# Low parts of the weights on VectorE, a float32 copy of the S5 result, head squares on TensorE, and q, k, g of the second sequence projected later

## The chip, the cores and the metric

The kernel runs on one core of a Trainium2 chip. The engines are TensorE (PE, its weight loads shown as PEld), VectorE (DVE), ScalarE (ACT), GpSimd (POOL) and SyncE (SP), which issues all the DMA transfers of this kernel. The metric is the device time of one execution in microseconds; less is better.

## What is computed

A trunk of two layers is applied to two sequences of 1024 rows and 1024 features with shared weights. All matrices are float32.

```python
def run(x):
    h = rmsnorm(x, norm_w[0])                       # layer 0
    z, xbc, dt_raw, q, k, v, g = split(h @ w_in_ab)
    y_ssd = ssd_mixer(z, xbc, dt_raw, ...)          # bidirectional, chunks of 128
    y_att = diff_attention(q, k, v, g, ...)         # 8 heads, two softmax maps each
    x = x + concatenate([y_ssd, y_att]) @ w_out_ab
    h = rmsnorm(x, norm_w[1])                       # layer 1
    u, zc = split(h @ w_in_c)
    y = gelu(s5(u))                                 # bidirectional complex scan
    y = y * sigmoid(y @ w_glu + b_glu)
    x = x + (y * silu(zc)) @ w_out_c
    return rmsnorm(x, final_norm_w)
```

In `diff_attention` each head's output is divided by the root of its mean square over 128 features (`o = rmsnorm(o, subln_w)`); that is the place of the squares below.

## The kernel before

**Dense products.** A float32 operand is kept as two parts, a rounded high part (`wh`, `ah`) and the remainder (`wl`, `al`), and a product is the sum of three: high by high, high by low, low by high. `load_w` (line 259) brings a block of 1024 x 512 weights in eight tiles `raw`; ACT makes `wh`, and POOL makes `wl` by a subtraction (line 277), except in the first half of the out-projection, where the weights are scaled and DVE makes it (`split`). With `cols=True` (`w_in_c`, `w_glu`) `raw` is read with a stride. One output tile `dn` of 128 x 512 is 24 matmuls, one block of weights 8 such tiles, 192 matmuls. Activations lie in eight tiles of the tag `act` (names `ac`), 1 MB each; one stage's input fills all of them, and the next stage's load (`load_half`) waits until tiles come free. In `mm_fm` both halves of the rows are in use up to the last column block of the last weights; in `mm_tm` the first half is done earlier.

**Two streams.** `run` (line 1399) writes the work in program order as dense blocks (`with P(bufs, pool)`) and vector stages (`V(...)`). The vector stages get a high priority (VPRIO): setup of the S5 matrices and tables, SSD and heads of sequence one, SSD and heads of sequence two, S5 of one (`s50`, with a low priority), S5 of two (`s51`). They follow each other in the same memory. The dense stream is: in-projection of one (`proj_fm`, `proj_qk` with z, q, k, g, `proj_v`), in-projection of two, out-projection of one (`out0`, a part for the SSD half and one for the attention half), `proj_1` of one, out-projection and `proj_1` of two, then `glu` and `out1` of one, `glu` and `out1` of two. Its results go through staging tiles `ev` of the pools `evd` (5 buffers), `evg` (EVG = 8 buffers, for `glu` and `out1` of one) and `pj`. Buffers of a tag are handed out in the order in which the program makes the tiles.

**The planner.** `Plan` (line 1525) takes all instructions, finds their dependences, and makes one order for each engine by a list schedule with its own costs: at every step the ready instruction with the least priority number goes first. `bonus` (line 1610) takes 10^7 off the number of an instruction that is not on PE and touches a tile `dn_`, `raw_`, `wh_` or `wl_`, so evictions of `dn` and weight preparation go ahead of the vector stages. Each engine then runs its order as it is written, and waits where an input is not there.

**The heads.** For each pair of 128-row blocks `head` (line 761) multiplies by V into `pv` (tag with one buffer), copies it to `oT`, transposes it into a second `pv`, squares the two halves on ACT with an accumulated sum (`sumsq`, tile `junk`), and copies it to `oall`. POOL adds the two softmax maps (`e<-e,e`).

**S5 and the gate.** `s5_unit` (line 1269) handles pairs of groups; after every fourth pair it applies the GELU, splits the result into `wr` and `wl` (which overwrites `w`), and stores both parts to `hT`. `glu` (line 1313) loads both parts as its matmul input, and for each output tile takes three `ev` tiles `y`, `z`, `th`: POOL adds the two parts again into `y` and multiplies by `z`, ACT makes `th` from `dn`, DVE multiplies `y` by it (line 1334) and splits it for the store to `yc`.

Of the kernel before, what the change touches and what calls it, by code (L numbers as in the profile page):

```python
# [27 lines left out]
VPRIO = 1000000  # L28
EVD, EVS, EVG = 5, 6, 8
EB, ACOMB = 4, 2  # L30
HFAST = True
# [23 lines left out]
class Kern:  # L55
# [86 lines left out]

    def rsqrt(self, pool, src, n, mul, add, extra=None, tag="rs", fast=False):

        nc = self.nc
        tag = self.cur["px"] + tag
        x = pool.tile([128, n], F32, tag=tag + "x", name=self.nm("rsx"), bufs=2)
        i_ = pool.tile([128, n], I32, tag=tag + "i", name=self.nm("rsi"), bufs=2)
        y = pool.tile([128, n], F32, tag=tag + "y", name=self.nm("rsy"), bufs=2)
        u = pool.tile([128, n], F32, tag=tag + "u", name=self.nm("rsu"), bufs=2)  # L150
        if extra is None:
# [106 lines left out]

    def load_w(self, w, c0, k0=0, rows=False, cols=False, scale=None, dve=()):


        hi, lo = [], []
        for k in range(8):
# [11 lines left out]
            if scale is None:  # L275
                self.act(hv, raw)
                self.tt(lv, raw, hr, AL.subtract, None if k in dve else self.nc.gpsimd)
            else:
                self.split(raw, hv, lv, scale[:, k:k + 1])
# [152 lines left out]
    def scratch(self, s):  # L432
# [15 lines left out]
        for b in range(8):  # L448
            d["u", b] = self.dt_([8, 16, 8, 128], f"u{s}_{b}")
            d["hT", b] = self.dt_([2, 8, 16, 8, 128], f"hT{s}_{b}")  # L450
        d["hg"] = [[[d["hT", b][x].rearrange("t c i x -> (c i) t x")[:, 4 * hf:4 * hf + 4, :] for b in range(8)]
                    for x in range(2)] for hf in range(2)]
# [72 lines left out]

    def proj_qk(self, s, sl, d):

        w = self.i["w_in_ab"][0]
        for which, c0 in (("z", Z0), ("q", Q0), ("k", K0), ("g", G0)):
            for blk in range(2):  # L530
                ww = self.load_w(w, c0 + blk * 512)
# [229 lines left out]
    def head(self, s, h, d, hp):  # L761
# [30 lines left out]
        for half in range(2):  # L792
# [4 lines left out]
            for t4 in range(4):  # L797
# [43 lines left out]
                for kt in range(8):  # L841
# [5 lines left out]
                    self.mm(pv[:, 0:256], vl, wh, False, kt == 7)  # L847
                oT = hp.tile([128, 256], F32, tag="oT", name=self.nm("oT"), bufs=1)
                self.act(oT, pv[:, 0:256])
                po = self.psv()  # L850
                for t2 in range(2):
                    self.tp(po[:, t2 * 128:t2 * 128 + 128], oT[:, t2 * 128:t2 * 128 + 128])
                for t2 in range(2):
                    self.sumsq(po[:, t2 * 128:t2 * 128 + 128], ssq[:, t4 - 1 + t2:t4 + t2])
                self.act(oall[:, t4 - 1:t4 + 1, :].rearrange("p a b -> p (a b)"), po[:, 0:256])
                if t4 == 1:
                    self.flush()
# [3 lines left out]
    def head_out(self, d, h, half, oall, ssq, s0, hp):  # L861
# [5 lines left out]
        self.stt(s2, sh, EPS, sh, AL.mult, AL.mult)  # L867
        r = self.rsqrt(hp, ssq, 4, 1.0 / 128.0, None, extra=s2, tag="hr", fast=HFAST)
        self.tt(oall, oall, r.unsqueeze(2).to_broadcast([128, 4, 128]), AL.mult)
# [399 lines left out]
    def s5_unit(self, a, q, U, d, sp, between):  # L1269

        nc = self.nc
        for k in range(8):
# [14 lines left out]
            if k % 4 == 3:  # L1287
                for gp in range(2):
                    w = self.ev()
                    self.act(w, ps[gp], AF.Square, scale=math.sqrt(0.044715))  # L1290
                    self.stt(w, w, 1.0, ps[gp], AL.add, AL.mult)
                    self.act(w, w, AF.Tanh, scale=math.sqrt(2.0 / math.pi))
                    self.stt(w, w, 1.0, ps[gp], AL.add, AL.mult)
                    wr, wl = self.ev(F32R), w.bitcast(F32R)
                    self.act(wr, w)
                    self.tt(wl, w, wr.bitcast(F32), AL.subtract)
                    for x, part in enumerate((wr, wl)):
                        self.dma(d["hT", a * 4 + gp * 2 + q][x].rearrange("t c i x -> (t c) i x")[:, k - 3:k + 1, :],
                                 part.rearrange("p (i x) -> p i x", x=128))
# [13 lines left out]
    def glu(self, s, d, big=None):  # L1313
# [7 lines left out]
        for nb in range(2):  # L1321
            ww = self.load_w(self.i["w_glu"][0], nb * 512, rows=True, cols=True)
            for t in range(8):
                hf, cb = t // 4, t % 4
                kf = nb * 4 + cb
                hh, hl = (a[:, cb, :].bitcast(F32) for a in sl[nb][hf])
                y, z, th = self.ev(), self.ev(), self.ev()
                self.dma(z, d["zT", kf][:, hf * 4:hf * 4 + 4, :].rearrange("p t c -> p (t c)"))
                self.tt(y, hh, hl, AL.add, g)
                self.tt(y, y, z, AL.mult, g)  # L1330
# [68 lines left out]
    def run(self):  # L1399
# [12 lines left out]
        @contextmanager  # L1412
        def P(bufs, pool):
            with self.stream(False, pool, bufs):
                yield
# [75 lines left out]
        with work("evd", "right") as ep:  # L1491
# [8 lines left out]
            with P(EVD, ep):  # L1500
                self.s5_T()
                D0(1, self.load_slots(d[1]["xT"]))
                self.out0(0, d[0], 0, xs[0])
            V("ssd1", SS(1))
            with P(EVD, ep):
                self.out0(0, d[0], 1, xs[0], h0)
                self.proj_1(0, d[0], h0)
# [17 lines left out]
class Plan:  # L1525
# [6 lines left out]
    LATE = (250, 0, 0, 0, 0)  # L1532
    DMA0, DMAR, ISSUE = 2300, 0.24, 420

    def __init__(self, tc, nc):
# [74 lines left out]
    def bonus(self, x, acc):  # L1610

        return 10 ** 7 if str(x.engine) != "EngineType.PE" and any(a[0].startswith(("dn_", "raw_", "wh_", "wl_")) for a in acc) else 0

# [258 lines left out]
```

## Time and profile before

| | us |
|---|---|
| median of 3 runs | 3622.99 (3618.75 to 3625.93) |
| profiled execution, its time | 3619.63 |
| profiled execution, its span | 3617.9 |

The span is the time from the first to the last instruction, the time has a little around it. The stages overlap; by the issues of their transfers the vector stages stand about here:

| stage of the vector stream | us from the start | dense work beside it |
|---|---|---|
| S5 matrices and tables | 150 to 570 | in-projection of one |
| SSD of one | 570 to 1015 | in-projection of one and two |
| heads of one | 1015 to 1600 | q, k, g, v of two |
| SSD of two | 1600 to 2050 | out-projection of one, start of `proj_1` |
| heads of two | 2050 to 2650 | `proj_1` of one, out-projection of two |
| S5 of one | 2650 to 2970 | out-projection of two, `proj_1` of two |
| S5 of two | 2975 to 3252 | end of `proj_1` of two, start of `glu` of one |
| none | 3252 to 3618 | `glu` and `out1` of one, then of two |

A row of the stages shows for each engine its busy time and the number of instructions, then PEclk, the TensorE clock that was granted as a share of 2.4 GHz, the mean busy share of the 16 DMA engines and what they moved. A row of a group shows the line, engine, operation, output and inputs, shape and count, then the busy time and the mean of one in ns, then the idle time of the engine before it with what ended that. A row of the timeline shows start, length, engine, instruction and how many of it in a row, in brackets the idle time before it.

### The profile page before, as it was taken

The page shows a single profiled execution, that of the slowest core. Times are in us where ns is not written, and L with a number is a line of the kernel's source. Part 1 is how long each engine was busy: PE and PEld are TensorE (multiplying, and loading weights), DVE is VectorE, ACT ScalarE, POOL GpSimd, SP SyncE. Part 2 cuts the span into 40 slices and gives each one's busy share as a digit, 9 for nine tenths or more (in the row PEclk, how much of TensorE's full clock was granted, in tenths as well). Part 3 has the DMA queues.
Part 4 walks back from the last instruction along what each step waited for, and adds up shares of the span by engine and source line. Part 5 has one row for each costly group of instructions (what it writes and reads, how often), then busy time and mean ns, then how long its engine had stood idle before and what let it go on. Part 6 is the DMA issues. An engine that isn't in the chain of part 4 may idle for free.

```text
span 3617.9 us, 52707 instructions
## 1 busy us (share of the span) xinstructions
PE 3291.4 (91%) x17206; PEld 2678.9 (74%) x17206; DVE 2605.3 (72%) x5393; ACT 1887.7 (52%) x3563; POOL 1019.6 (28%) x781
## 2 busy tenths in 40 slices
PE   6999999999999999998987899999897998659899
PEld 5776788767778888886666678888676787557677
DVE  5488888767857776767788757777758967983243
ACT  4333323447657777744466577776645555443231
POOL 2121223121224444430010144433411112115471
PEclk9999999999999999999997999999998999779999
DMA  5646766886656555449986465686387659758752
GB/s 191 167 136 190 239 209 207 305 285 218 185 158 186 173 172 170 145 155 329 304 282 218 137 168 155 185 243 191 120 277 234 208 186 286 228 186 276 205 171 70
DMA packets 609619, 737.34 MB, mean 204 GB/s; under 512 B 104409, under 2 KB 374361, under 8 KB 609305
## 3 DMA queue, kind: packets, MB, share of 16 engines
q1 hardware_dynamic: 609344, 733.98, 64.8%
q8 instruction: 137, 2.24, 0.3%
q14 instruction: 138, 1.12, 0.1%
HBM read 491.57 MB, written 246.42 MB: 204 GB/s over the span
## 4 chain that ended last, share of the span: by engine, by line
PE 64%; DVE 12%; DMA 6%; ACT 4%; issue 3%; POOL 2%; SPq 1%; DVEq 0%; POOLq 0%; ACTq 0%
PE dn L113 44%; PE q L113 8%; PE pv L113 5%; PE tr L131 3%; PE tr L113 2%; DVE m L116 2%; DMA raw<-in_w_in_ab_dram 2%; DVE b L116 2%; POOL wl L116 1%; SPq L110 1%; DVE E L119 1%; DVE m L1257 1%; DMA raw<-in_w_in_c_dram 1%; PE pv L131 1%; ACT ev L128 1%
## 5 line engine op out<-in xcount | busy, mean ns | idle before, releaser
L113 PE MATMUL dn<-ac,wh 128*128 128x512 f32 x4288 | 1390.7, 401 | 41.1 <-ACT wh L128 26.8
L116 POOL TENSOR_TENSOR wl<-raw,wh 128x512 fp32r<-128x512 f32 x368 | 550.7, 1511 | 1544.1 <-PE dn L113 861.7
L113 PEld LDWEIGHTS dn<-ac,wh 128*128 128x128 f32 x4288 | 806.8, 191 | 223.8 <-ACT wh L128 32.8
L113 PE MATMUL dn<-ac,wl 128*128 128x512 f32 x2144 | 853.8, 401 | 10.6 <-POOL wl L116 10.5
L113 PE MATMUL dn<-wh,ac 128*128 128x512 f32 x1792 | 586.1, 403 | 37.4 <-DVE ev L116 21.0
L113 PEld LDWEIGHTS dn<-ac,wl 128*128 128x128 f32 x2144 | 407.1, 190 | 110.1 <-POOL wl L116 22.4
L128 ACT ACTIVATE e<-e,st 128x1024 f32<-128x1024 f32 x384 | 437.8, 1150 | 67.7 <-DVE st L820 43.3
L116 POOL TENSOR_TENSOR e<-e,e 128x1024 f32<-128x1024 f32 x128 | 308.2, 2408 | 513.0 <-ACT e L128 400.6
L113 PEld LDWEIGHTS dn<-wh,ac 128*128 128x128 f32 x1792 | 341.8, 193 | 122.3 <-DVE ev L116 25.3
L128 ACT ACTIVATE wh<-raw 128x512 fp32r<-128x512 f32 x368 | 274.8, 752 | 263.7 <-DMA raw<-in_w_in_ab_dram 125.0
L128 ACT ACTIVATE ev<-dn 128x512 f32<-128x512 f32 (+2 forms) x252 | 157.3, 627 | 406.2 <-PE dn L113 394.8
L113 PE MATMUL dn<-wl,ac 128*128 128x512 f32 x896 | 361.9, 405 | 3.4 <-DVE wl L119 1.6
L113 PE MATMUL q<-K,Q 128*128 128x512 f32 x1024 | 315.7, 407 | 4.7 <-DVE st L820 3.0
L820 DVE CUSTOM_DVE_ANT_0 e<-q,Tb 128x512 f32<-128x512 f32 x256 | 175.2, 684 | 85.2 <-PE q L113 52.4
L820 DVE CUSTOM_DVE_ANT_0 e<-q,Tb,st 128x512 f32<-128x512 f32 x256 | 191.3, 747 | 38.2 <-PE q L113 20.0
L116 DVE TENSOR_TENSOR wT<-tr,wT 128x512 fp32r<-128x512 f32 x256 | 171.2, 685 | 64.0 <-ACT wT L128 63.3
L113 PE MATMUL pv<-wT,V 128*128 128x256 f32 x1536 | 207.9, 284 | 0.5 <-ACT wT L128 0.3
L113 PEld LDWEIGHTS q<-K,Q 128*128 128x128 f32 x1024 | 179.5, 190 | 38.3 <-DVE st L820 8.1
L113 PEld LDWEIGHTS pv<-wT,V 128*128 128x128 f32 x1536 | 198.9, 190 | 10.4 <-ACT wT L128 1.2
L113 PEld LDWEIGHTS dn<-wl,ac 128*128 128x128 f32 x896 | 172.7, 193 | 45.5 <-POOL wl L116 5.0
L128 ACT ACTIVATE wT<-tr 128x512 fp32r<-128x512 f32 x256 | 149.4, 597 | 100.5 <-PE tr L131 99.2
L128 ACT ACTIVATE G<-P,dt 128x128 f32<-128x128 f32 x512 | 158.7, 389 | 28.1 <-DVE dt L119 10.4
(287 smaller groups left out, 4872.6 us busy)
## 6 DMA issues: line engine op xcount, KB each, us to landing
raw<-in_w_in_ab_dram SPq DMA_DIRECT2D x208, 256.0 KB
Q<-q SPq DMA_DIRECT2D x512, 64.0 KB
tab<-TAB SPq DMA_DIRECT2D x64, 384.0 KB
Tb<-bh_d SPq DMA_DIRECT2D x32, 704.0 KB
q<-ev SPq DMA_DIRECT2D x64, 256.0 KB
k<-ev SPq DMA_DIRECT2D x64, 256.0 KB
v<-ev SPq DMA_DIRECT2D x64, 256.0 KB
ab<-acs SPq DMA_DIRECT2D x32, 512.0 KB
```

Of the source, the lines that this page charges most:

```text
L110: self.nc.sync.dma_start(out=out, in_=in_)
L113: self.nc.tensor.matmul(out, lhsT=l, rhs=r, start=start, stop=stop)
L116: (eng or self.nc.vector).tensor_tensor(out=out, in0=a, in1=b, op=op)
L119: self.nc.vector.scalar_tensor_tensor(out=out, in0=a, scalar=sc, in1=b, op0=op0, op1=op1)
L128: self.nc.scalar.activation(out=out, in_=in_, func=func, **kw)
L131: self.nc.tensor.transpose(out, in_, self.ident[:n, :n])
L820: nc.vector.tensor_tensor_reduce(out=et[:, kc], in0=sp, in1=Tb[:, x0 + kh * 512:x0 + kh * 512 + 512], op0=AL.add, op1=AL.min, scale=1.0, s ...
L1257: nc.vector.tensor_tensor_scan(out=fl(m[:, x]), data0=fl(tab[:, 2]), data1=fl(b[:, x]), initial=0.0, op0=AL.mult, op1=AL.add)
```

## The change

`wl` is made on DVE for all weights. The S5 result is also stored in float32 (`hf`), with `wl` in a tile of its own, and `glu` loads it in place of the addition on POOL. In the heads POOL squares `oT` into `o2`, PE sums its columns with a vector of ones into two spare columns of the transposed tile, and ACT copies the sums. The in-projection of sequence two is split: `proj_fm`, z and v come first, then the SSD half of the out-projection of one; the input is loaded again, and q, k, g follow, written behind the SSD of two. EVG is 14 in place of 8, a helper's small tiles in the heads have one buffer in place of two, and the planner's `bonus` also holds for every instruction not on PE that touches a tile of `evd`, `evg` or `pj`.

```diff
-EVD, EVS, EVG = 5, 6, 8
+EVD, EVS, EVG = 5, 6, 14
 ...
                 self.act(hv, raw)
-                self.tt(lv, raw, hr, AL.subtract, None if k in dve else self.nc.gpsimd)
+                self.tt(lv, raw, hr, AL.subtract)
 ...
+            d["hf", b] = self.dt_([8, 16, 8, 128], f"hf{s}_{b}")
 ...
-    def proj_qk(self, s, sl, d):
+    def proj_qk(self, s, sl, d, what="zqkg"):
 ...
         for which, c0 in (("z", Z0), ("q", Q0), ("k", K0), ("g", G0)):
+            if which not in what:
+                continue
 ...
-                oT = hp.tile([128, 256], F32, tag="oT", name=self.nm("oT"), bufs=1)
+                oT, o2 = (hp.tile([128, 256], F32, tag="oT", name=self.nm("oT"), bufs=2) for _ in range(2))
                 self.act(oT, pv[:, 0:256])
+                self.tt(o2, oT, oT, AL.mult, g)
 ...
                 for t2 in range(2):
-                    self.sumsq(po[:, t2 * 128:t2 * 128 + 128], ssq[:, t4 - 1 + t2:t4 + t2])
+                    self.mm(po[:, 256 + t2:257 + t2], o2[:, t2 * 128:t2 * 128 + 128], self.ones[:, 0:1], True, True)
                 self.act(oall[:, t4 - 1:t4 + 1, :].rearrange("p a b -> p (a b)"), po[:, 0:256])
+                self.act(ssq[:, t4 - 1:t4 + 1], po[:, 256:258])
 ...
-                    wr, wl = self.ev(F32R), w.bitcast(F32R)
+                    wr, wl = self.ev(F32R), self.ev(F32R)
                     self.act(wr, w)
                     self.tt(wl, w, wr.bitcast(F32), AL.subtract)
-                    for x, part in enumerate((wr, wl)):
-                        self.dma(d["hT", a * 4 + gp * 2 + q][x].rearrange("t c i x -> (t c) i x")[:, k - 3:k + 1, :],
+                    blk = a * 4 + gp * 2 + q
+                    for dst, part in ((d["hT", blk][0], wr), (d["hT", blk][1], wl), (d["hf", blk], w)):
+                        self.dma(dst.rearrange("t c i x -> (t c) i x")[:, k - 3:k + 1, :],
                                  part.rearrange("p (i x) -> p i x", x=128))
 ...
-                hh, hl = (a[:, cb, :].bitcast(F32) for a in sl[nb][hf])
                 y, z, th = self.ev(), self.ev(), self.ev()
-                self.tt(y, hh, hl, AL.add, g)
+                self.dma(y.rearrange("p (t x) -> p t x", x=128),
+                         d["hf", kf].rearrange("t c i x -> (c i) t x")[:, t4, :])
                 self.tt(y, y, z, AL.mult, g)
 ...
-                D0(1, self.load_slots(d[1]["xT"]))
+                s1 = self.load_slots(d[1]["xT"])
+                self.proj_fm(1, s1, d[1])
+                self.drain(self.proj_qk(1, s1, d[1], "z"))
+                self.proj_v(1, s1, d[1])
                 self.out0(0, d[0], 0, xs[0])
             V("ssd1", SS(1))
             with P(EVD, ep):
+                s1 = self.load_slots(d[1]["xT"])
+                self.drain(self.proj_qk(1, s1, d[1], "qkg"))
                 self.out0(0, d[0], 1, xs[0], h0)
 ...
+    DENSE = ("_evd_", "_evg_", "_pj_")
 ...
     def bonus(self, x, acc):
-        return 10 ** 7 if str(x.engine) != "EngineType.PE" and any(a[0].startswith(("dn_", "raw_", "wh_", "wl_")) for a in acc) else 0
+        if str(x.engine) == "EngineType.PE":
+            return 0
+        for a in acc:
+            t = self.tiles.get(a[0])
+            if a[0].startswith(("dn_", "raw_", "wh_", "wl_")) or t is not None and any(
+                    k in str(t.cap_key) for k in self.DENSE):
+                return 10 ** 7
+        return 0
```

## Rows read from the trace of the kernel before

**Rows 1.** Page, part 1: busy us, share of the span, instructions.
```profile
PE 3291.4 (91%) x17206; PEld 2678.9 (74%) x17206; DVE 2605.3 (72%) x5393; ACT 1887.7 (52%) x3563; POOL 1019.6 (28%) x781
```
**Rows 2.** Stages: PE, PEld, DVE, ACT, POOL busy (count), clock, DMA share, GB/s.
```profile
1015.00:1600.00 585.00, 577.03 (x3203) 493.36 (x3202) 408.39 (x1082) 406.37 (x781) 246.39 (x140) 1.00 0.54 165
...
1800.00:2050.00 250.00, 200.54 (x1135) 153.78 (x1136) 214.85 (x422) 152.03 (x339) 39.05 (x24) 0.85 0.73 232
...
2650.00:2940.00 290.00, 259.89 (x1400) 221.46 (x1399) 247.49 (x417) 159.32 (x253) 47.24 (x30) 0.94 0.73 237
...
3070.00:3236.00 166.00, 93.72 (x482) 84.15 (x482) 154.99 (x270) 75.50 (x125) 12.19 (x8) 0.74 0.65 211
3236.00:3440.00 204.00, 179.32 (x730) 141.69 (x731) 70.58 (x97) 60.74 (x102) 107.08 (x164) 0.92 0.76 239
3440.00:3618.00 178.00, 167.70 (x719) 135.63 (x718) 74.47 (x146) 48.31 (x86) 78.63 (x62) 0.98 0.36 118
```
**Rows 3.** Waits of POOL from 3070 to 3250: us in total, times, longest.
```profile
POOL ev L116 <- DMA yc<-ev: 145.0, 1, 145.0
```
**Rows 4.** Timeline of the second S5: single lines of ACT, DVE and SP.
```profile
3086.67 1.27 ACT L128 ACTIVATE ev<-dn,gb 128x512 f32<-128x512 f32 x2 [2.39 <-PE dn L113]
...
3238.11 1.28 DVE L119 SCALAR_TENSOR_TENSOR ev<-ev,ev 128x512 f32<-128x512 f32 x2
...
3251.58 0.45 SPq L110 DMA_DIRECT2D hT<-ev  x1
```
**Rows 5.** Stages of the tile `dn` alone: PE, PEld, (DVE,) ACT busy (count).
```profile
3070.00:3236.00 166.00, 14.24 (x54) 10.32 (x54) 0.00 (x0) 1.27 (x2) 0.74 0.65 211
...
3437.00:3618.00 181.00, 169.82 (x722) 136.94 (x722) 10.97 (x16) 10.88 (x16) 0.97 0.38 121
```
**Rows 6.** Timeline near 440 and 460: POOL's low parts and DVE's table products.
```profile
439.21 5.12 POOL L116 TENSOR_TENSOR wl<-raw,wh 128x512 fp32r<-128x512 f32 x3 [3.38 <-ACT wh L128]
439.73 1.77 DVE L116 TENSOR_TENSOR tab<-tab 128x512 f32<-128x512 f32 x1
...
460.44 0.69 DVE L116 TENSOR_TENSOR tmp<-tab 128x512 f32<-128x512 f32 x1
```
**Rows 7.** Stages of the tile `m` on DVE alone: busy (count), clock, DMA.
```profile
2650.00:2940.00 290.00, 167.65 (x271) 0.94 0.73 237
3100.00:3236.00 136.00, 98.66 (x187) 0.73 0.60 194
```
**Rows 8.** Groups of DVE, 2650 to 2940, then 3100 to 3236: a PSUM reader.
```profile
L119 DVE SCALAR_TENSOR_TENSOR ev<-ev,q 128x512 f32<-128x512 f32 x28 | 19.1, 683 | 6.1 <-ACT ev L128 6.0
...
L119 DVE SCALAR_TENSOR_TENSOR ev<-ev,q 128x512 f32<-128x512 f32 x20 | 13.6, 681 | 1.1 <-ACT ev L128 1.1
```
**Rows 9.** Groups of the whole span, shapes kept apart: busy us, mean ns.
```profile
L116 POOL TENSOR_TENSOR wl<-raw,wh 128x512 fp32r<-128x512 f32 x368 | 550.7, 1511 | 1544.1 <-PE dn L113 861.7 <-ACT wh L128 375.4 <-issue 142.4
...
L119 DVE SCALAR_TENSOR_TENSOR uz<-ev,dn 128x512 f32<-128x512 f32 x16 | 17.1, 1079 | 28.5 <-ACT ev L128 28.3
```
**Rows 10.** Stages of POOL's low parts `wl`: POOL busy (count), clock, DMA.
```profile
150.00:1015.00 865.00, 184.25 (x120) 0.98 0.67 211
1800.00:2050.00 250.00, 39.05 (x24) 0.85 0.73 232
2650.00:2940.00 290.00, 47.24 (x30) 0.94 0.73 237
```
**Rows 11.** Group of the squares in the heads, whole span.
```profile
L128 ACT ACTIVATE junk<-pv 128x128 bf16<-128x128 f32 x128 | 34.9, 273 | 8.4 <-PE pv L131 6.0
```
**Rows 12.** Timeline near 768: one-column matmuls on PE.
```profile
768.23 1.05 PE L113 MATMUL tr<-ones,zh 128*128 128x1 f32 x8 [0.25 <-ACT zh L128]
```
**Rows 13.** Stages with the fullest DMA, columns as in the stages above.
```profile
1750.00:1850.00 100.00, 83.05 (x423) 57.99 (x422) 76.84 (x141) 45.03 (x100) 13.31 (x8) 0.91 0.96 321
...
3050.00:3100.00 50.00, 36.35 (x185) 29.71 (x185) 39.57 (x51) 21.33 (x32) 21.51 (x13) 0.86 0.98 290
```
**Rows 14.** Chain that ended last, 2300 to 2360: start, us, what.
```profile
2332.86 12.57 DMA ac<-ys
```

More of the change, by code (lines that the diff above doesn't have):

```diff
@@ L141, in c4, with rsqrt @@
         return t
-    def rsqrt(self, pool, src, n, mul, add, extra=None, tag="rs", fast=False):
+    def rsqrt(self, pool, src, n, mul, add, extra=None, tag="rs", fast=False, bufs=2):
         nc = self.nc
         tag = self.cur["px"] + tag
[L147 to L150, printed above, removed]
+        x = pool.tile([128, n], F32, tag=tag + "x", name=self.nm("rsx"), bufs=bufs)
+        i_ = pool.tile([128, n], I32, tag=tag + "i", name=self.nm("rsi"), bufs=bufs)
+        y = pool.tile([128, n], F32, tag=tag + "y", name=self.nm("rsy"), bufs=bufs)
+        u = pool.tile([128, n], F32, tag=tag + "u", name=self.nm("rsu"), bufs=bufs)
         if extra is None:
@@ L257, in tick, with load_w @@
             self.queue.pop(0)()
-    def load_w(self, w, c0, k0=0, rows=False, cols=False, scale=None, dve=()):
+    def load_w(self, w, c0, k0=0, rows=False, cols=False, scale=None):
         hi, lo = [], []
@@ L867, in head_out @@
         self.stt(s2, sh, EPS, sh, AL.mult, AL.mult)
-        r = self.rsqrt(hp, ssq, 4, 1.0 / 128.0, None, extra=s2, tag="hr", fast=HFAST)
+        r = self.rsqrt(hp, ssq, 4, 1.0 / 128.0, None, extra=s2, tag="hr", fast=HFAST, bufs=1)
         self.tt(oall, oall, r.unsqueeze(2).to_broadcast([128, 4, 128]), AL.mult)
@@ L1325, in glu @@
                 kf = nb * 4 + cb
-                hh, hl = (a[:, cb, :].bitcast(F32) for a in sl[nb][hf])
                 y, z, th = self.ev(), self.ev(), self.ev()
-                self.dma(z, d["zT", kf][:, hf * 4:hf * 4 + 4, :].rearrange("p t c -> p (t c)"))
-                self.tt(y, hh, hl, AL.add, g)
+                t4 = slice(hf * 4, hf * 4 + 4)
+                self.dma(z, d["zT", kf][:, t4, :].rearrange("p t c -> p (t c)"))
+                self.dma(y.rearrange("p (t x) -> p t x", x=128),
+                         d["hf", kf].rearrange("t c i x -> (c i) t x")[:, t4, :])
                 self.tt(y, y, z, AL.mult, g)
```

## The prediction

> **What bounds the kernel now.** I read the shares of busy time first [rows 1]: PE is busy in 91% of the span, DVE in 72%, ACT in 52%, POOL in 28%. An average over stages with different limits says little, so the second view is the table of stages [rows 2]. Three kinds of stage stand in it. In the first sequence's heads (1015 to 1600) PE is busy 577 of 585 us at clock 1.00: every cycle added to PE there is paid, and nothing else is. In the second SSD and in the first S5 (1800 to 2050 and 2650 to 2940) DVE is the fullest engine (215 of 250, 247 of 290). And from 3070 to 3236 PE is busy 94 of 166 us at a granted clock of 0.74, while DVE is at 155 of 166. That last stage is the odd one: work for PE is there, since `glu` and `out1` of sequence one still stand ahead, but of their matmuls only 54 run in it [rows 5].
>
> The waits say why [rows 3]: POOL waits once for 145.0 us until a store `yc<-ev` has landed. The timeline gives the chain [rows 4]: the two first tanh evictions of `glu` run on ACT at 3086.67, but the next step of the same tiles, the multiplication on DVE (line 1334), starts only at 3238.11, when the second S5 has almost left the queue. `bonus` (line 1612) lifts only instructions that touch `dn_`, `raw_`, `wh_` or `wl_`; the eviction reads `dn`, the multiplication and the split after it touch `ev` alone, so the plan put them behind all of the S5's DVE work. With 8 buffers and three `ev` tiles for each step the third step gets none, and PE stands still as far as `glu` goes for as long.
>
> **The change part by part.** The sum is made against the profiled execution: its span is 3617.9, its time 3619.6, and the median of the runs shown, 3623.0, lies 3.4 above that.
>
> *The planner's bonus for `ev` tiles, EVG 14.* The multiplication and the split of `glu` now go ahead of the S5 on DVE, so `glu` and `out1` of sequence one (4 blocks of 192 matmuls, 768 less the 54 already run) move into the stage that starts at 3070. What is late next? DVE: the second S5 needs the 182 us until its last store at 3251.58 [rows 4], and the moved blocks bring 32 evictions of `glu` and 48 of `out1` at 0.69 [rows 6], 55 us, and 32 low parts (below), 28 us: 265 us, the end at 3335. PE: 714 matmuls at 169.82/722 = 0.235 us [rows 5] are 168 us, and the S5's 79 us at clock 0.74 [rows 2, 5] are 59 at full clock, 65 for 182 us: 233 us, so PE is not the bound. DMA: 0.65 of 182 us for the S5 and 0.76 of the 188 us that are left of the next stage [rows 2] are 118 + 143, and the change adds 8.4 MB here (16 stores and 16 loads of 256 KB), 26 us at 211 GB/s per 0.65: 287 us of full engines. The fullest rows show 0.96 and 0.98 [rows 13], so 302 us at 0.95: the end at 3372. DMA ends last by this, DVE 37 us before it. Then comes the tail that needs the second S5: 181 us for `glu` and `out1` of sequence two [rows 5] and about 8 us for the last store and load. 3372 + 189 = 3561 against 3618 is a gain of 57, with the DVE end instead 94. I take 60, near the DMA end, because 0.98 was measured right in this place, from 3050 to 3100.
>
> The same bonus reaches the stores, loads and norm steps of the other dense stages. From 1800 to 2050 PE idles 49 us [rows 2]; the DVE time there is needed all the same, so I count 10 us of it and bound it by 0 and 35.
>
> *Low parts on DVE.* 368 instructions leave POOL, 1.51 us each in the mean [rows 9]. On DVE 272 of them cost the 0.69 of a 128x512 instruction from SBUF, and 96 with a strided side (the input of `w_in_c` and `w_glu`) 1.08, as `uz<-ev,dn` takes it [rows 9]; the trace has no such subtraction on DVE, and the bounds are 0.69 and the 1.51 of POOL. That is 188 + 104 = 292 us more for DVE. Against it stands what POOL takes from DVE now: with POOL on low parts a `tab` instruction takes 1.77, without 0.69 [rows 6]. The two S5 stages measure it: from 2650 to 2940 POOL is busy 47 us [rows 2] with 30 low parts [rows 10], and the instructions on `m` take 167.65/271 = 0.619; with POOL empty they take 98.66/187 = 0.528 [rows 7]. 271 x 0.091 = 25 us, 0.82 per low part, is given back against 0.69 to 1.08 paid. In the stages that DVE limits I count nothing; elsewhere PE covers it, and if that cover goes it is some 30 us in each stage of heads. The Trainium skill, SBUF — State Buffer, "Who interferes with whom", says that VectorE with two inputs in SBUF and a GpSimd instruction that reads SBUF share a read interface, and that the loser blocks for the whole instruction. The trace agrees in kind: `ev<-ev,q`, which reads PSUM, takes 0.683 beside POOL and 0.681 without [rows 8]. By that rule each low part could give back its whole 1.51 us, 45 us instead of 25 in that stage.
>
> *Squares on PE.* ACT loses 128 squares of 273 ns with their accumulator reads [rows 11], 35 us and more, and gets 64 small copies. POOL gets 64 products of 128x256, some 0.75 us each if half of a low part. PE gets 128 matmuls of one column; eight of that shape take 1.05 us [rows 12], 0.13 each: 17 us at most. Half of them fall in the heads where PE has 8 us idle, and count: +8, bounds 0 and 17. New waits: PE's column matmul waits for POOL, where the heads' additions `e<-e,e` of 128x1024 stand ahead; `psv` has one buffer, so the next product with V waits behind it. Low parts that no longer stand on POOL pay for that; 0.
>
> *S5 result also in float32.* 32 additions leave POOL in `glu`, 32 loads and 32 stores of 256 KB come on SP's queue and are counted in the DMA sum for sequence one; for sequence two the load lies under PE work (DMA share 0.36 from 3440 on [rows 2]). The separate low tile takes three of the S5's six `ev` buffers in place of two, used once in four pairs of groups; 0.
>
> *q, k, g of sequence two later.* 6 blocks go behind `out0(0,0)`: 48 weight loads, 80 stores and their evictions change places with 16 weight loads, 16 loads and 16 stores, and SP issues 8 more loads (8.4 MB) of the normalised input. Against: the reload lies in the heads, where DMA is at 0.54 [rows 2]; but the handover from `g` to the attention half is now of the kind where both halves of the input are in use until the last column block, as at 2332.86, where the load of `ys` holds the chain for 12.57 us [rows 14]: +12. For: where `out0(0,0)` stands now DMA is at 0.96 [rows 13], and the load of `ys` with `out0`'s traffic (21 MB) gives way to the stores of k and g (15 MB); 6 MB at 321 GB/s are 19 us, of which I count 10. Net +2, bounds -18 and +15. The heads of sequence two read q, k and g only after the SSD that begins then, so nothing waits for them.
>
> Sum: -60 - 10 + 0 + 8 + 2 = -60; 3619.6 - 60 = 3559.6, and 3.4 up to the median is 3563, rounded to **3560**, with 3525 to 3600 for this case by the bounds.
>
> **The rivals.** (a) DMA does not bind the overlapped stage and the bonus fills the SSD stage too: 34 us and 25 us more, 3500. For it: 0.95 is my figure, the rows go to 0.98. Against: DVE is at 86% in that SSD already, and the plan never packs every transfer. (b) DVE becomes the bound: in the stages to 1015, from 1800 to 2050 and from 2650 to 2940 stand 120 + 24 + 30 = 174 low parts [rows 10], and the V work (S5 setup, SSD, S5) has to wait for each. If little comes back from POOL, 174 x 0.79 (292/368) = 137 us lengthen the chain, and the kernel ends near 3700, slower. It decides from a relief under 0.45 us per low part on, where 174 x 0.34 eats the 60; rows 7 measure 0.82 for one stage. (c) The starvation stays: the float32 load stands late in SP's order, or the three tiles are still handed out in turn and the S5 keeps DVE. Then 60 are missing: 3620. Against it: rows 4 name the instruction, and it now has the bonus. (d) Each low part on POOL holds DVE for all of its 1.51 us [rows 9], so the same 174 give back 0.69 more each than rows 7 say, 120 us: 3440. The lock on the page SBUF — State Buffer of the Trainium skill ("Who interferes with whom") would give that. Rows 7 speak against it.
>
> **How the numbers follow.** Chances: the forecast 0.61, (a) 0.17, (b) 0.09, (c) 0.09, (d) 0.04. The range from 3485 to 3615 takes in the forecast, most of (a), and leaves out (b), (d) and most of (c). Faster by over 0.2% (what a measurement of this kernel can tell from no change) is the forecast, (a), (d) and a third of (c): 0.85; slower is (b): 0.09; 0.06 remain.
>
> **What would show it.** Right: in the second S5 the matmuls of `dn` run through, the 145 us wait of POOL is gone, DMA there is above 0.9, the clock above 0.9; DVE's `m` instructions take 0.53 in both S5; POOL is busy under 600 us. Wrong: the second S5 ends before 3300 or after 3420; `dn` waiting for DVE's `wl` for tens of us; `tr` or `pv` in the heads waiting for POOL's product; strided low parts near 1.5 us. What makes the forecast wrong most easily is the plan itself: it is made anew from all priorities, and every queue's order with it.

## The result and the profile after

The changed kernel takes 3524.5 us in the median (3520.9 to 3532.3), the kernel before, run beside it, 3623.8: a ratio of 0.9731, 95% interval 0.9712 to 0.9750. The forecast was 3560 with a range from 3485 to 3615. The gain is 99 us where 60 were forecast; the time lies inside the range, and the sections below are about the other 39 us. The profiled execution has a span of 3519.1 us, 98.8 under that of before.

The shares of busy time of the changed kernel, to be held against [rows 1]:

```profile
PE 3284.7 (93%) x17462; PEld 2677.3 (76%) x17462; DVE 2652.7 (75%) x5761; ACT 1859.3 (53%) x3371; POOL 483.3 (14%) x445
```

PE has 256 matmul records more and is busy 7 us less; POOL has lost more than half of its work; DVE has taken 368 instructions and is busy only 47 us more. Span less PE's busy time is PE's idle time: 326.5 us before, 234.4 after. So 92 of the 99 us are idle time of PE, and the tables below are read with that sum.

The stages of the changed kernel (columns as in [rows 2]): heads of one, second SSD, first S5, second S5, tail. Each stretch is cut at this kernel's own loads and stores, so that it is the same work as the stage of before, at another time:

```profile
974.00:1574.00 600.00, 590.57 (x3312) 503.32 (x3312) 435.60 (x1147) 385.86 (x669) 194.52 (x112) 0.99 0.61 191
1756.00:2004.00 248.00, 223.98 (x1285) 171.57 (x1285) 207.60 (x440) 154.94 (x364) 0.00 (x0) 0.91 0.77 246
2616.00:2928.00 312.00, 282.92 (x1502) 239.48 (x1502) 269.17 (x477) 172.10 (x271) 0.59 (x6) 0.93 0.73 240
2931.00:3332.00 401.00, 339.29 (x1716) 284.71 (x1714) 311.29 (x516) 184.41 (x300) 59.89 (x120) 0.93 0.92 299
3332.00:3519.00 187.00, 173.89 (x738) 139.93 (x738) 79.68 (x167) 47.91 (x86) 24.33 (x24) 0.97 0.43 135
```

The same cut in the kernel before gives 2970 to 3252 for the second S5 and 366 us of tail. The tile `dn` alone, of before (first fence, those two stretches) and after:

```profile
2970.00:3252.00 282.00, 97.49 (x385) 71.25 (x384) 11.72 (x11) 9.73 (x16) 0.83 0.74 235
3252.00:3618.00 366.00, 335.06 (x1405) 267.47 (x1403) 21.93 (x32) 18.32 (x27) 0.96 0.58 182
```

```profile
2931.00:3332.00 401.00, 266.85 (x1076) 199.36 (x1074) 23.83 (x28) 18.01 (x28) 0.93 0.92 299
3332.00:3519.00 187.00, 173.89 (x738) 139.93 (x738) 11.05 (x16) 10.96 (x16) 0.97 0.43 135
```

That is the starvation of [rows 5], gone: 1076 dense matmuls run beside the second S5 in place of 385, at a clock of 0.93 in place of 0.83, and the tail is 187 us, with 189 forecast. But the whole vector chain also stands earlier: the first S5 load is issued at 2616 instead of 2652 us. The forecast's terms for what lies ahead of the S5 (-10, +8 and +2) add up to nothing. Here it is in the SP lines of before and of after:

```profile
2651.67 0.49 SPq L110 DMA_DIRECT2D mi<-MIN  x1
```

```profile
2615.95 0.32 SPq L110 DMA_DIRECT2D mi<-MIN  x1
```

### The profile page after: what moved, and what is told of

The parts are those of the page before. It is cut to its first block, busy times and chain, and to the rows that moved or that the text cites. A ratio compares the mean times of both kernels' runs of the same rounds, so it can differ in the third digit from the quotient of the medians.

```text
span 3519.1 us, 52816 instructions
## 1 busy us (share of the span) xinstructions
PE 3284.7 (93%) x17462; PEld 2677.3 (76%) x17462; DVE 2652.7 (75%) x5761; ACT 1859.3 (53%) x3371; POOL 483.3 (14%) x445
## 4 chain that ended last, share of the span: by engine, by line
PE 70%; DVE 13%; DMA 7%; ACT 5%; issue 3%; SPq 1%; POOL 0%; DVEq 0%; ACTq 0%; POOLq 0%
PE dn L113 48%; PE q L113 9%; PE pv L113 5%; PE tr L131 4%; PE tr L113 2%; DMA raw<-in_w_in_ab_dram 2%; DVE wl L116 2%; ACT wh L128 1%; DVE m L116 1%; DVE b L116 1%; PE pv L131 1%; SPq L110 1%; DVE E L119 1%; ACT ev L128 1%; DVE ev L119 1%
## 5 line engine op out<-in xcount | busy, mean ns | idle before, releaser
L116 DVE TENSOR_TENSOR wl<-raw,wh 128x512 fp32r<-128x512 f32 x368 | 290.9, 801 | 119.2 <-ACT wh L128 78.8
L113 PE MATMUL q<-K,Q 128*128 128x512 f32 x1024 | 325.5, 409 | 2.8 <-DMA Q<-q 1.1
```

The costliest lines, as they stand in the source:

```text
L113: self.nc.tensor.matmul(out, lhsT=l, rhs=r, start=start, stop=stop)
L116: (eng or self.nc.vector).tensor_tensor(out=out, in0=a, in1=b, op=op)
```

## The experiments

The disputed steps are four: whether the low parts on VectorE cancel (term 0), what the bonus does outside the second S5 (term -10), the squares (term +8), and whether the transfers bound the overlapped stage. "S5 start" below is the issue of the first `mi<-MIN`, "tail" the time from the last `hT` store to the end. Each run had its own executions of the kernel before beside it, whose medians lie between 3625.2 and 3627.5; the interval given is that of the ratio to them. By these intervals a difference under some 10 us between two runs is not settled.

### Low parts: undone, alone, twice, on both engines

Undone in the changed kernel:

```diff
-                self.tt(lv, raw, hr, AL.subtract)
+                self.tt(lv, raw, hr, AL.subtract, self.nc.gpsimd)
```

> The changed kernel with one edit undone: all 368 low parts of the weight blocks are computed by GpSimd again, none by VectorE. Theory A (the low parts on VectorE are what lets the vector chain reach the S5 stage 39 us earlier, 2611 us instead of 2650, because a VectorE operation that runs beside a GpSimd one is held): the first S5 operation comes back to about 2650, the excess of VectorE from GpSimd overlap rises from about 102 us towards 303, and the time is 3550 to 3585 us. Theory B, that of the prediction (what VectorE gains by the relief it pays back by executing the low parts, term 0; the 39 us come from the bonus and the moved projections): S5 still starts within 10 us of 2611 and the time is 3515 to 3535 us.

Measured: 3570.6 us (0.9845, 0.9824 to 0.9866), 46 over the changed kernel, S5 start 2652. All three signs of theory A are there; the excess of VectorE beside GpSimd, explained below, is 286 us.

The kernel before with that one edit in the other direction (`None if k in dve else self.nc.gpsimd` taken out of line 277):

> The kernel before with one edit: all low parts on VectorE. Theory A (low parts bring the vector chain forward by about 39 us): S5 starts at 2605 to 2625 us instead of 2650, the second S5 half still starves the dense work (the wait of dn there stays), and the time is 3570 to 3600 us. Theory B (the prediction's term 0: relief equals cost): S5 starts within 10 us of 2650 and the time is 3610 to 3635 us.

Measured: 3566.5 us (0.9833, 0.9818 to 0.9847), 59 under before, S5 start 2610. The time lies 3.5 us under theory A's range, which is within the noise. Its tail is still 366 us (3200 to 3566), so the starvation is untouched. Theory A holds in both directions: the low parts bring the vector chain forward. Theory B, the prediction's zero, falls.

Then the two prices by themselves. In the changed kernel each low part a second time on VectorE:

```diff
                 self.tt(lv, raw, hr, AL.subtract)
+                self.tt(lv, raw, hr, AL.subtract)
```

> The changed kernel with a cost doubled: each of the 368 low parts is computed twice by VectorE, one after the other into the same tile, some 291 us of VectorE more. The prediction's step held that this work and the relief from GpSimd cancel because VectorE binds, so the cost C of one set of low parts on VectorE would be near 200 us of path or more: 3700 to 3815 us. Theory A' (the low parts mostly fill VectorE's idle time beside the dense work, while a GpSimd operation holds up whatever VectorE has, the short operations of the chain too): C is 10 to 70 us, so 3534 to 3594 us, and the relief is C plus the 46 us that separate the kernel with the low parts on GpSimd from the changed one.

Measured: 3759.1 us (1.0362, 1.0344 to 1.0379). One set of low parts on VectorE costs 3759 - 3524 = 235 us of path. So theory A' falls: these instructions do not sit in idle time. The prediction's view that VectorE binds in most places where they stand holds. And once more on GpSimd instead (`self.tt(lv, raw, hr, AL.subtract, self.nc.gpsimd)` as the second line):

> The changed kernel with all 368 low parts computed by VectorE and then once more, into the same tile, by GpSimd: the GpSimd work of before and the VectorE work of the changed kernel together. If the price of one set on VectorE (C = 235 us by the kernel that computes them there twice) and the price of one set on GpSimd (R, by what it takes from VectorE) add up, then R = C + 46 = 281 and the time is 3790 to 3820 us. If C is convex (the second set costs more than the first because the idle time of VectorE is used up by then), R is smaller: with R of 80 to 200 the time is 3600 to 3725 us. If GpSimd's work costs VectorE nothing and the 46 us were the shorter wait for the low part, 3560 to 3580 us.

Measured: 3806.5 us (1.0500, 1.0473 to 1.0527), 282 over the changed kernel, where the sum of the two earlier runs gave 281. The prices add up within the noise: a set of low parts costs 282 us on GpSimd and 235 on VectorE. The short wait for a low part as the only cause, the third case, is excluded: it wanted 3560 to 3580. How long TensorE waits for a low part stands in these rows (us in total, times, longest), of the changed kernel, the one with the low parts on GpSimd, the one with both sets on VectorE, and the one with a set on either engine:

```profile
PE dn L113 <- DVE wl L116: 9.6, 6, 4.5
...
PE dn L113 <- POOL wl L116: 14.5, 27, 2.0
...
PE dn L113 <- DVE wl L116: 38.4, 45, 3.6
...
PE dn L113 <- POOL wl L116: 54.5, 52, 4.0
```

Undoing the edit lengthens this wait by 5 us, of the 46. In the two kernels with a second set it is longer by 29 and 45 us. So that much of the 235 and of the 282 is a wait for the later result and not time taken from VectorE; some 206 and 237 are left.

The groups of the low parts show where GpSimd's price is paid. The changed kernel, the kernel with both sets on VectorE, and the kernel with a set on either engine (busy us, mean ns | idle before, releaser):

```profile
L116 DVE TENSOR_TENSOR wl<-raw,wh 128x512 fp32r<-128x512 f32 x368 | 290.9, 801 | 119.2 <-ACT wh L128 78.8 <-PE dn L113 35.1 <-DMA mi<-MIN 1.2
```

```profile
L116 DVE TENSOR_TENSOR wl<-raw,wh 128x512 fp32r<-128x512 f32 x736 | 582.1, 809 | 122.7 <-ACT wh L128 68.4 <-PE dn L113 41.0
```

```profile
L116 POOL TENSOR_TENSOR wl<-raw,wh 128x512 fp32r<-128x512 f32 x368 | 589.8, 1611 | 1661.0 <-DVE wl L116 806.8 <-ACT ev L128 211.9 <-ACT G L128 160.6
L116 DVE TENSOR_TENSOR wl<-raw,wh 128x512 fp32r<-128x512 f32 x368 | 381.6, 1049 | 143.3 <-ACT wh L128 94.3 <-PE dn L113 36.1 <-DMA V<-v 4.6
```

The same 368 VectorE instructions take 290.9 us alone and 381.6 beside GpSimd's. I summed, over all VectorE instructions that overlap one on GpSimd, what each takes above the median of its shape without overlap: 102 us in the changed kernel and 405 with a set on either engine, 303 / 368 = 0.82 us for each GpSimd low part. [rows 7] gave the same value from the instructions on `m` in one stage.

PE pays twice for added waiting. With both sets on VectorE its 17462 matmuls are the same, but:

```profile
PE 3364.7 (90%) x17462; PEld 2717.7 (72%) x17462; DVE 2957.0 (79%) x6129; ACT 1864.5 (50%) x3371; POOL 478.7 (13%) x445
```

Of 239 us more span 159 are idle time of PE, and 80 are the same matmuls taking longer, the mean granted clock being 0.943 instead of 0.965.

### The bonus: taken out, alone, for one pool alone, with fewer buffers

```diff
-    DENSE = ("_evd_", "_evg_", "_pj_")
+    DENSE = ()
```

> The changed kernel without the scheduling bonus for the evd, evg and pj tiles (the evg pool still has 14 buffers). The prediction's theory (the bonus is what keeps the second S5 half from starving the dense work): between the second half's start and its last store the dn matmuls are few again, the tail after the last hT store is near 350 us instead of 187, and the time is 3584 to 3625 us (60 to 100 more than 3524). Rival (the 14 buffers or the earlier vector chain do it alone): the tail stays below 220 us and the time is 3520 to 3545 us.

Measured: 3593.5 us (0.9907, 0.9892 to 0.9922), 69 over the changed kernel. The tile `dn` in this kernel's second S5 and tail:

```profile
2941.00:3226.00 285.00, 116.53 (x457) 85.69 (x457) 12.80 (x12) 11.86 (x19) 0.84 0.80 255
3226.00:3591.00 365.00, 327.91 (x1355) 260.27 (x1354) 22.02 (x32) 17.08 (x25) 0.94 0.63 199
```

It is the starvation of before again, buffers or not, so the prediction's theory holds in the changed kernel. What nobody expected is the S5 start: 2565 us, 51 earlier than with the bonus. The bonus delays the vector chain.

The kernel before with the bonus and the 14 buffers alone:

> The kernel before with the bonus for the three tile groups and the evg pool of 14 buffers, and nothing else of the change. The prediction's theory (the bonus carries the gain, all other parts sum to zero): 3550 to 3570 us. Theory A (the bonus removes the starvation of the second S5 half only, the 39 us of earlier S5 need the low parts on VectorE): S5 starts at 2640 to 2655 us, the end lies 55 to 65 below before, also near 3560; so the start of S5 tells the two apart from theory C (the bonus brings both, S5 starts near 2611 and the time is 3515 to 3535 us).

Measured: 3608.6 us (0.9952, 0.9934 to 0.9971), a gain of 17. The S5 starts at 2676, 24 later than before; the stretch from there to its last store grows from 600 to 745 us, the tail falls from 366 to 186. The tail is what was forecast, and most of what it gains is lost ahead of it. None of the three theories said so. Between this run and the first one (3571), which adds the other edits but not the low parts, lie 38 us that no run divides. They are the squares, the move and the float32 copy together; undone in the changed kernel, below, the same three come out as a loss of 17. So what a part is worth depends on the others.

The bonus for `evg` alone, on top of the kernel with the squares on ScalarE (3495 us, below):

```diff
-    DENSE = ("_evd_", "_evg_", "_pj_")
+    DENSE = ("_evg_",)
```

> The kernel with the squares on ScalarE again (3495 us), and the bonus for the evg tiles alone, not for evd and pj. Theory (the evg part ends the starvation in the second S5 half, while the evd and pj parts delay the vector chain ahead of it, 2565 against 2616 us for the first S5 operation without and with the bonus): S5 starts 20 to 50 us earlier than 2589, the tail after the last S5 store stays near 187 us, and the time is 3455 to 3485 us. Rival (what the vector chain gains, the dense work loses, since PE is at 93%): S5 starts earlier, the stretch to its last store grows as much, and the time is 3490 to 3520 us.

Measured: 3467.0 us (0.9566, 0.9543 to 0.9589), S5 start 2571, tail 189. The S5 starts 18 us earlier, just short of the 20 expected, and the stretch from there to its last store doesn't grow, as the rival has it, but falls from 716 to 701 us. So the `evd` and `pj` parts of the bonus cost 28 us, and the `evg` part alone ends the starvation. This is the fastest kernel of the study, 160 us under before and 57 under the change:

```profile
PE 3237.8 (94%) x17206; PEld 2638.4 (76%) x17206; DVE 2664.3 (77%) x5761; ACT 1887.4 (55%) x3563; POOL 438.6 (13%) x381
```

The buffers (`EVG` 14 to 8, also on the kernel of 3495 us):

> The kernel with the squares on ScalarE again (3495 us), and 8 buffers in the evg pool instead of 14, the bonus as in the changed kernel. If the 14 buffers are needed for the dense work to run through the second S5 half: its last store comes 10 us or more later or the tail grows, 3510 to 3560 us. If the bonus alone does it: 3488 to 3502 us.

Measured: 3503.2 us (0.9657, 0.9632 to 0.9682). The interval overlaps that of the kernel with 14 (0.9624 to 0.9652), and the time lies between the two ranges, so whether six buffers are worth 8 us is not settled; the bonus does nearly all of it.

### The squares

The edit puts `sumsq` on ScalarE back in place of the product `o2` on GpSimd, the two matmuls with a column of ones, and the copy of their result (`oT` has one buffer again):

```diff
-                self.tt(o2, oT, oT, AL.mult, g)
...
-                    self.mm(po[:, 256 + t2:257 + t2], o2[:, t2 * 128:t2 * 128 + 128], self.ones[:, 0:1], True, True)
+                    self.sumsq(po[:, t2 * 128:t2 * 128 + 128], ssq[:, t4 - 1 + t2:t4 + t2])
...
-                self.act(ssq[:, t4 - 1:t4 + 1], po[:, 256:258])
```

> The changed kernel with one edit undone: the squares of the heads are summed on ScalarE with an accumulating activation again, not by a GpSimd product and two matmuls. The prediction's step (squares on PE cost +8, between 0 and 17): 3507 to 3524 us, the heads of both sequences (600 and 600 us long in the changed kernel) shorter by up to 20 us each, GpSimd busy about 100 us less. Rival (ScalarE's relief in the heads pays for it): 3530 us or more.

Measured: 3495.0 us (0.9638, 0.9624 to 0.9652), 29 under the changed kernel, more than the step's upper bound of 17. The rows of the changed kernel say why:

```profile
L113 PE MATMUL pv<-ones,oT 128*128 128x1 f32 x256 | 32.2, 229 | 0.0
```

The program makes 128 such matmuls, and 256 records stand in the trace: two for each. I had read [rows 12], eight records in 1.05 us, as eight matmuls, and so counted half. With PE busy 93% of the time most of the 32 us is paid: without them PE's busy time falls by 40 us, from 3284.7 to 3244.9, its idle time grows by 14, and the span falls by 26. The heads of one, where PE hardly idles, fall from 600 to 585 us, half of the 32; those of two, from their start to the S5's, only from 612 to 604:

```profile
970.00:1555.00 585.00, 576.96 (x3196) 492.04 (x3195) 438.21 (x1146) 400.98 (x765) 175.88 (x84) 0.99 0.63 196
```

ScalarE has room for its 128 squares, since it is busy 401 of these 585 us. The edit also takes 64 products from GpSimd. No run undoes them alone, but they hold VectorE up little: the excess of VectorE beside GpSimd, summed as for the low parts, is 102 us with them and 107 without.

### The move and the float32 copy

`D0(1, ...)` in one go again, and the reload of the normalised input with `proj_qk(..., "qkg")` gone from behind `out0(0, d[0], 0, ...)`:

> The changed kernel with one edit undone: q, k and g of sequence two are projected again in one go with z and v, ahead of the first half of the out-projection. The prediction's step (the move costs +2, between -18 and +15): 3507 to 3540 us, S5 still starting within 15 us of 2616. Rival (the move is one of the sources of the gain, because it gives the heads of sequence one dense work that is ready): 3545 us or more, with more PE idle between 1574 and 2004 us.

Measured: 3535.9 us (0.9756, 0.9738 to 0.9773), 11 over the changed kernel, the two intervals overlapping. S5 start 2636, 20 us later where at most 15 were expected. The second SSD is 265 us long without the move and 248 with it, and PE waits there and just ahead of it for VectorE's `y` for 16.4 us instead of 1.8. If it is a gain, it is a small one, within the step's bounds (-18 to +15), on the other side of its +2.

The gate's input from the two parts again, 16.8 MB less in all (762.5 to 745.7); the store of the copy and the separate low tile are gone too:

```diff
-                self.dma(y.rearrange("p (t x) -> p t x", x=128),
-                         d["hf", kf].rearrange("t c i x -> (c i) t x")[:, t4, :])
+                self.tt(y, hh, hl, AL.add, g)
```

> The changed kernel with one edit undone: the S5 result is not stored in float32 for the gate; GpSimd adds its two parts again, and the 8.4 MB written and 8.4 MB read for the copy are gone. If the DMA bounds the second S5 half, as the prediction took it (its end near 3372 by the DMA): the last store of the S5 result falls from 3332 to 3305 or earlier, and the time to 3500 to 3515 us. Rival (VectorE bounds that stretch, or the dense work that fills it; the transfers are hidden, and the GpSimd sums hold VectorE up instead): the last store stays within 10 us of 3332 and the time is 3518 to 3540 us.

Measured: 3525.5 us (0.9721, 0.9707 to 0.9736), no difference, last S5 store at 3329, as the rival has it. Its second S5:

```profile
2933.00:3329.00 396.00, 344.84 (x1735) 288.38 (x1734) 316.16 (x503) 185.38 (x301) 68.29 (x96) 0.93 0.87 277
```

DMA falls from 0.92 to 0.87 and the stretch keeps its length within 5 us. Had the transfers bound it, it would have been shorter, unless the GpSimd sums that came back cost the same; with 16 sums in the stretch at 0.82 that is 13 us at most, and the excess of VectorE in the stretch grows by 9 us (15 to 23), against 26 us of transfers. DMA as the bound of the whole stretch is not supported; for a part of it, where its share is 0.93 to 0.97 (2928 to 3250), it is not excluded. What does bound it is not settled: PE idles 62 us there in the changed kernel, 34.5 of them for ScalarE's `X`, a link of the S5's own chain:

```profile
PE q L113 <- ACT X L128: 34.5, 9, 12.0
PE dn L113 <- ACT wh L128: 13.2, 4, 10.8
```

### The price carried to another operation

If GpSimd takes from VectorE in proportion to its time, the heads' sums should go to VectorE too (on the kernel of 3467 us):

```diff
-EB, ACOMB = 4, 2
+EB, ACOMB = 4, 0
```

> The kernel of 3467 us (squares on ScalarE, bonus for evg alone) with one step of the heads on VectorE: the 128 sums of the two attention maps, now a scaling copy on ScalarE (1.15 us each) and a GpSimd addition of 128x1024 (2.41 us each, 308 us in all), become one VectorE operation each (about 1.22 us, as the product ce of the same shape takes, 156 us in all). Theory R (GpSimd's work takes from VectorE in proportion to its time, 281 us per 555 us as with the low parts, so 156 us come back for 156 paid): the heads keep their length within 10 us and the time is 3450 to 3480 us. Rival (what GpSimd holds up depends on what VectorE executes meanwhile: in the heads that is mostly operations that read PSUM, which take 0.684 beside GpSimd as without it, so little comes back): VectorE's busy time rises by 100 us or more, the heads get 10 to 50 us longer each unless PE covers it, and the time is 3485 to 3560 us.

Measured: 3523.3 us (0.9703, 0.9683 to 0.9723), 56 slower. Theory R falls. VectorE gets 164 us of sums and is busy 72 us more, so 92 us come back for 308 us of GpSimd, 0.30 per us, where the low parts gave back 0.82 per 1.6. The rival has the time right, and its premise: in the heads VectorE mostly reads PSUM, and those instructions are not held up. But it wanted VectorE's busy time to rise by 100 us or more, so more came back than it said. Of the kernel with the sums on GpSimd:

```profile
L823 DVE CUSTOM_DVE_ANT_0 e<-q,Tb 128x512 f32<-128x512 f32 x256 | 175.1, 684 | 46.2 <-PE q L113 23.9 <-POOL e L116 18.2 <-PE tr L131 3.8
```

and with them on VectorE:

```profile
L823 DVE CUSTOM_DVE_ANT_0 e<-q,Tb 128x512 f32<-128x512 f32 x256 | 174.6, 682 | 12.7 <-PE q L113 12.4
L119 DVE SCALAR_TENSOR_TENSOR e<-e,st,e 128x1024 f32<-128x1024 f32 x128 | 164.3, 1284 | 4.1
```

0.682 against 0.684. The Trainium skill, SBUF — State Buffer, "Who interferes with whom", says that a VectorE instruction with at most one input in SBUF, outside its 2-port modes, does not contend with GpSimd; these rows agree. The place of the loss is not the one the rival named. The heads of one are 15 us longer (591 for 576). Those of two, from their start to the S5's, are shorter (570 for 612), but PE idles 47 us there instead of 18, mostly to wait for the sums:

```profile
PE tr L131 <- DVE e L119: 28.2, 11, 5.4
```

Dense work is left over there. Here are the matmuls of `dn` in the heads of two and in the first S5, of the kernel with the sums on GpSimd, then with them on VectorE:

```profile
1959.00:2571.00 612.00, 352.14 (x1328) 0.99 0.62 181
2571.00:2880.00 309.00, 203.03 (x777) 0.94 0.74 243
```

```profile
1987.00:2557.00 570.00, 250.88 (x964) 0.97 0.56 163
2557.00:2934.00 377.00, 300.82 (x1155) 0.96 0.75 248
```

The loss shows up in the first S5, 377 us long where it was 309. It takes the 364 matmuls that are missing in the heads of two, and it begins with 63 us in which PE is full and VectorE hardly works (20.9 of 63 us, where the other kernel's first S5 begins with 47.3 of 63):

```profile
2557.00:2620.00 63.00, 63.00 (x288) 52.43 (x287) 20.93 (x32) 9.02 (x14) 0.00 (x0) 1.00 0.80 273
```

That the waits for the sums are why the plan leaves these matmuls to that place is argued; it was not tried.

## Why the prediction was right, and where it was not

Undone one at a time in the changed kernel, the five parts give: low parts -46, bonus with its evictions -69, squares +29, move -11, float32 copy -1, in sum -98, with -99 measured. That the sum fits so well is luck. Each term is good to some 10 us (worked out from the ratios instead of the medians, the five give -77), and the parts don't simply add: for the S5 start the same sum, in the same order (-37 +51 +27 -20 -3), gives 18 us later, where the change brought it 36 us forward. So the terms hold for the changed kernel, one edit at a time.

The prediction's terms for the five were 0, -70, +8, +2 and 0, in sum -60. It named the largest part with its size there, though the bonus and the buffers alone gain 17 on the kernel before. By these terms the difference of 39 us is three of them: low parts 46 too high, move 13 too high, squares 21 too low. So the errors partly cancel. The time lies nearer to rival (a), 3500, than to 3560, but not by its mechanism: the way from the S5's first load to its last store is as long as forecast, and the bonus delays the vector chain ahead of it.

**Bonus and 14 buffers (-60 and -10).** The total is right in the changed kernel, its parts are not. The starvation and its cause are those of [rows 3 to 5]: it is back when the bonus is taken out. The tail is 187 us as forecast. But the "-10 elsewhere" has the wrong sign. It is +28 for `evd` and `pj`, measured on the kernel with the squares on ScalarE, since the S5 then starts later by 18 us and takes 15 us more; that this comes from evictions put ahead of the vector chain on VectorE is argued, as the bonus holds for all engines but PE. If the two add up, some -97 are left for `evg`, an estimate across two kernels.

**The end of the second S5 (3372 by DMA, 3335 by VectorE).** It came at 3332. From the S5's first load on that is 716 us, and the forecast's 3372 - 2652 is 720. The length is right and its reason is not supported: with the transfers of the copy gone the stretch stays as it is. That the estimate at 0.95 of DMA came out is then partly luck; the true bound is open. The VectorE estimate, 3335, is hit only because the S5 began 36 us earlier.

**Low parts (0).** The step's parts were all read well: the busy time is 290.9 us against a forecast of 292; strided ones take about 1.05 us and contiguous ones 0.69, as two single ones of the changed kernel show:

```profile
2711.47 1.05 DVE L116 TENSOR_TENSOR wl<-raw,wh 128x512 fp32r<-128x512 f32 x1
...
1617.49 0.69 DVE L116 TENSOR_TENSOR wl<-raw,wh 128x512 fp32r<-128x512 f32 x1 [1.78 <-ACT wh L128]
```

and the relief is 0.82 for each. `m` in the first S5 takes 155.36/288 = 0.539 us, against 0.619 in [rows 7]; with the low parts back on GpSimd it is 0.617:

```profile
2616.00:2928.00 312.00, 155.36 (x288) 0.93 0.73 240
```

```profile
2652.00:2973.00 321.00, 177.72 (x288) 0.95 0.72 235
```

What failed is setting the difference to zero. On the path the relief is worth 282 / 368 = 0.77 us for each low part and the cost 235 / 368 = 0.64, and 368 times 0.13 is some 47 us, where undoing the edit gave 46. Both prices hold the longer waits for the second result, 45 and 29 us, so each is an upper bound. Two numbers of some 290 us were written down as equal, one of which (0.82 of relief) came back nearly whole on the path, and the other (0.79 of cost) did not; a fifth of it, 56 of 291 us, costs nothing. That this fifth stands beside idle time of VectorE is argued. The rivals (b) and (d) went the two wrong ways from there: (b) took the relief away, (d) the whole 1.51 us as relief; 0.77 to 0.82 is what the runs show.

**Squares (+8, 0 to 17).** Mis-sized at one place: each of these one-column float32 matmuls leaves two records, so 17 should have been 32, and most of it is on the path, not half. The count of the group in the kernel before would have said so, beside the 128 matmuls `tr<-ones,zh` of the program:

```profile
L113 PE MATMUL tr<-ones,zh 128*128 128x1 f32 x256 | 34.9, 257 | 15.5 <-ACT zh L128 15.4
```

The wait for POOL's product, which the prediction named, doesn't show: PE stands idle 0.0 us ahead of the group `pv<-ones,oT`.

**Move (+2) and float32 copy (0).** The move is within its bounds, the copy at its 0. With the move the second SSD starts 19 us earlier and is 17 us shorter, the way from there to the S5 is 16 us longer, and some 11 us remain. Which of the two arguments in its step this bears out is not shown.

**What was to be seen.** The dense matmuls run through, DMA in the second S5 is at 0.92, the clock at 0.93, POOL is busy 483 us. Not as said: `m` in the second S5 takes 0.58 (111.16/191), since GpSimd's gate products now run beside it; and POOL's wait of 145 us has a successor, 131.4 us for the load of the copy. It costs nothing that shows, since with the copy and its load gone the time is the same:

```profile
POOL ev L116 <- DMA ev<-hf: 188.7, 10, 131.4
```

## What to carry to other kernels

When an operation moves between GpSimd and VectorE, price both ends separately and keep the difference. Here a GpSimd operation cost VectorE nothing where VectorE read PSUM, and much where VectorE's two inputs lay in SBUF; so count those instructions, not GpSimd's busy time. Give evictions priority over a vector chain only in the pool that starves; here the same priority in the other pools delayed the chain and cost 28 us. Before a row's duration is divided by its count, see how many records one call of the program leaves: here it was two for each one-column matmul. And undo parts in the changed kernel as well as adding them to the old one: the bonus was worth 69 us in the one and 17 in the other.

## What was not expected of the hardware

The prices of the low parts are additive far beyond what a busy share of 75% suggests: 235 us for the second set on VectorE and 282 for a set on GpSimd, with VectorE then busy 78 to 79% of the span; the waits for the second result are 29 and 45 us of that. And waiting lengthens the matmuls themselves: the same 17462 matmul records take 3284.7 us at a mean granted clock of 0.965, 3364.7 at 0.943, and with a set on either engine:

```profile
PE 3375.4 (89%) x17462; PEld 2713.9 (71%) x17462; DVE 2949.3 (78%) x5761; ACT 1866.6 (49%) x3371; POOL 1065.4 (28%) x813
```

Busy time times clock is 3170 us in the first and 3173 in the second, so the clock accounts for the difference. From the changed kernel to the one in the row PE's idle time grows by 189 us (234.4 to 423.3) and its busy time by 91, so in these two kernels each us of added waiting cost about another half.
